# Two streams for the triangular inverses of an RWKV-7 mixer

## The chip, the cores and the metric

The kernel runs on one core of a Trainium2 chip. A core has a matrix engine (TensorE, PE), a vector engine (DVE), a scalar engine (ACT), GpSimd (POOL) and a queue engine (SyncE, SP); each takes its instructions in order and they meet at semaphores. The metric is the device time of one launch in microseconds, the median of three runs: 1651.26 us before the change.

## The reference, cut to what matters

One layer of a recurrent decoder: norm, one input projection, three mixers side by side on the channels, one output projection, norm, MLP, norm. There are 1024 prompt tokens and 8 sample tokens of 1024 channels. The change is in the first mixer, RWKV-7: 6 heads of 64 channels, each with a 64 x 64 state that is updated token by token.

```python
def step(S, inp):
    rt, wt, kt, vt, kkt, at = inp
    sa = jnp.einsum('bhvk,bhk->bhv', S, -kkt)
    S = S * wt[:, :, None, :] + sa[..., None] * (kkt * at)[:, :, None, :] + vt[..., None] * kt[:, :, None, :]
    return S, jnp.einsum('bhvk,bhk->bhv', S, rt)
```

The other two mixers are HGRN2 (6 heads, chunks of 64 tokens) and RG-LRU (a scan over 256 channels).

## The kernel before, in words

Tokens are worked in two halves of 512; the samples go with the second. All dense products take both operands split into two parts, three products for each.

**RWKV-7 in quarters.** Two heads (a pair, 128 channels) by 256 tokens are a *quarter*. There are 12: `PARTS` lists (pair j, half hf, quarter qt) with the half outermost, so quarters 2k and 2k+1 are neighbours in time of one pair, and even and odd quarters alternate. A quarter has four chunks of 64 tokens, and passes through four generators:

- `rw_operands(q)`: decay, removal key, scaled keys and queries (`ee`, `ar`, `kb`, `kbt`, `uv`) and the bonus `bo`. It announces `A2` when done (L565).
- `rw_inverse(q)`: the scores `sc` of the 8 blocks (chunk, head), and the inverse of a triangular 64 x 64 matrix for each, by doubling: five levels, each a product W (from `sc` and `xm`), a copy on ACT to `wm` (L615), a product Y (from `wm` and `ym`), a masked copy into `ym` (L630) and a transpose into `xm` (L634), both on DVE. At the end the product `mv` is copied into `xm` (L641), and `B` is announced. All its products go to two PSUM banks (`ra`).
- `rw_chain(q)`: four steps of the recurrence over the chunks; ends with the copy to `ot` (L700) and announces `C`.
- `rw_finish(q)`: group norm, bonus, gate; the last instruction is at L734, and `P` is announced.

The operands hold back by two announcements of the quarter two before and one of the quarter before:

```python
        if q >= 2:
            yield ("C", q - 2)          # L517
        if q >= 1:
            yield ("sc", q - 1)
        ...
        if q >= 2:
            yield ("P", q - 2)          # L555, just before the bonus
```

**The order of PE's instructions** is the order in which `weave` draws pieces from the generators. It keeps a rough clock of PE, `now`. A generator yields either a time until its next piece can start (the constants D1 to D42) or an announcement that it waits for. Of the ready streams the one that has waited longest is taken; the *filler*, which is the dense work, is taken only where no other stream is ready. Each stream has a priority in `PRI` that goes to the order on the other engines. The streams are the chain, the inverse, the operands, the finish, HGRN2 and the sample step, RG-LRU; each works its quarters one after the other, so only one inverse is under way at a time. The filler `projections()` projects the 27 column tiles of each half in the order of `ORDER`, then does the output projection of the first half, and as much of that of the second (two column tiles over six of eight mixers) as does not need the last mixers; the rest waits until all streams have ended. Six slots hold the projections of the RWKV mixer, three for a pair and a half, which the odd quarter of the pair gives back.

After that come the norm, and the MLP in eight blocks, where PE runs dense products to the end.

Of the kernel before, what the change touches and what calls it, by code (L numbers as in the profile page):

```python
# [9 lines left out]
F32 = mybir.dt.float32  # L10
# [5 lines left out]
PSUM = bass.MemoryType.PSUM  # L16

P = 128
# [22 lines left out]
PRI = [-100, 0, 300, 300, 300, 100, 300]  # L41
# [9 lines left out]
def kernel(ctx: ExitStack, tc: tile.TileContext, i, o):  # L51
# [13 lines left out]
    # The order of the tensor engine's instructions is the order of emission while streams are woven: `now` is a rough  # L65
    # clock of that engine, by which `weave` takes the stream whose operands should be there.
# [15 lines left out]
    def weave(streams, filler, to_the_end=False):  # L82
        """Emits the streams (generators) piece by piece. A stream yields the microseconds until its next piece can
        start, or what it waits for; the filler runs where no other stream is ready."""
# [52 lines left out]
    def x_cols(k, hf):  # L137
        """Where a half of the tokens of a channel tile waits: the mix is written later."""
        return mix[k][:, XC[hf][0]:XC[hf][0] + XC[hf][1]]
# [48 lines left out]
    # lower bound of the forget gate: cumsum(softmax over the depth) minus its first row  # L188
# [13 lines left out]
    # 2 softplus(-lam) = 2 (max(-lam, 0) + log1p(exp(-|lam|))), log1p(e) = 2 atanh(e / (2 + e))  # L202
# [25 lines left out]
    small = ctx.enter_context(tc.tile_pool(name="small", bufs=2))  # L228

    def inv_root(src, n, scale, eps, name):  # L230
        """[128, n] of 1/sqrt(scale * src + eps), src in PSUM."""
        a = small.tile([P, 32], F32, tag="ir", name=f"ir_{name}", bufs=4)
        V.tensor_scalar(a[:, :n], src, scale, eps, op0=ALU.mult, op1=ALU.add)
        rpow(a[:, :n])
        return a

    def head_inv_root(sq, n, name, tag, floor, tmp):
        """sq [128 channels (2 heads), n tokens] -> PSUM [128, n]: 1/sqrt of the sum per head and token."""
# [7 lines left out]
        # on every channel of the head, then channel-major  # L246
# [7 lines left out]
    def load_w(src, name, kt=KT, wpool=wpool, dst=None, parts=1):  # L254
        """One 128-column tile of a weight matrix as its two exact parts."""
# [9 lines left out]
    def dense_steps(out, wh, wl, xh, xl, ks=range(KT), first=True, last=True):  # L265
        """out (PSUM) = W^T x with both operands split in two parts; xh/xl: k -> AP."""
        n = 0
        for k in ks:
            for a, b in ((wh, xh), (wh, xl), (wl, xh)):
                mm(out, a[:, k, :], b(k), start=first and n == 0, stop=last and n == 3 * len(ks) - 1)  # L270
                n += 1
                if n % 2 == 0:
                    yield 0.0
# [16 lines left out]
    def warm(n):  # L290
        """Products that nobody reads: the tensor engine's clock comes up, and stays up, with work."""
# [4 lines left out]
    def norm1(hf):  # L296
        """RMS norm of a half of the tokens; the samples go with the second half. The first half is projected before its
        scale is known, which then falls to the projections; the second is scaled in place."""
# [44 lines left out]
    def xn_cols(hf):  # L343
        """The input of a half in two parts: without the scale of the token in the first, normalised in the second."""
# [8 lines left out]
    def shift_out():  # L353
        """Shift states: the last prompt token and the sample tokens after the norm."""
# [9 lines left out]
    def take(tag):  # L364
        """Waits until a slot of a tag that the projections fill and the mixers empty is free."""
# [10 lines left out]
    def next_w(ask=True):  # L376
        """The next tile of the weights in `ahead`; the one after it is asked for."""
# [5 lines left out]
    # the scale of the first half waits where the mixer of its last projections writes  # L383
# [3 lines left out]
    def project(hf, col, c0, n, bank="big"):  # L387
        """A column tile of a chunk of tokens."""
# [4 lines left out]
    def take_out(hf, out, pt):  # L393
        """A projection to SBUF."""
# [7 lines left out]
    def in_proj(hf, col, evac, shift=False):  # L402
        """Projects a column tile; the next tile's weights (in `ahead`) are asked for before."""
# [14 lines left out]
    def shifted(hf, col, name, out, tag, bufs):  # L418
        """out: pm = P + mu (P_prev - P) of one column tile."""
# [19 lines left out]
    # =========================================================================================  # L439
    # RWKV-7  # L440
    # =========================================================================================
# [37 lines left out]
    def units():  # L479
        """(chunk, head, rows, columns) of the 64 x 64 blocks of a quarter, column halves taking turns."""  # L480
# [4 lines left out]
    def rw_operands(q):  # L485
        """Decay, removal key, bonus and the operands of the scores of a quarter of the tokens of a pair of heads."""
# [15 lines left out]
        # normalised removal key  # L502
        act(t2, k_, AF.Square, scale=vec("kk", j))
        # decay and in-context learning rate
# [12 lines left out]
        if q >= 2:  # L517
            yield ("C", q - 2)
# [3 lines left out]
        ee = rwp.tile([P, NQ, C + 1], F32, tag="ee", name=f"ee_{n}", bufs=2)  # L522
        ar = rwp.tile([P, NQ, 2, C], F32, tag="ar", name=f"ar_{n}", bufs=2)
        kb = rwp.tile([P, NQ // 2, 4, C], F32, tag="kb", name=f"kb_{n}", bufs=1)
        kbt = rwp.tile([P, NQ, P], F32, tag="kbt", name=f"kbt_{n}", bufs=2)
        uv = rwp.tile([P, NQ, P], F32, tag="uv", name=f"uv_{n}", bufs=2)
# [3 lines left out]
        # values, token-major  # L530
# [18 lines left out]
        # token-major [K|B]  # L549
# [18 lines left out]
    def rw_inverse(q):  # L568
        """Scores and Y = (I - A B^T masked)^-T of every (chunk, head), by dyadic blocks."""
# [4 lines left out]
        # scores: rows [K;B] (even chunks) or [B;K] (odd), columns [A|R]  # L574
        sc = rwp.tile([P, 2 * NQ, P], F32, tag="sc", name=f"sc_{n}", bufs=2)
        ym, xm = (w2(nm, n).rearrange("p (u t) -> p u t", t=C) for nm in ("ym", "xm"))
# [21 lines left out]
        for l in range(1, 6):  # L598
            # the last level fills one 32 x 32 block of every unit
            last = l == 5  # L600
            wm = w2("wm", n, 1, f"wm{l}")
# [34 lines left out]
        # what the values of the chunk itself add, for every unit  # L636
# [9 lines left out]
    def rw_chain(q):  # L646
        """The recurrence over the chunks of a quarter; the state is block-diagonal over the two heads."""
# [6 lines left out]
        for c in range(NQ):  # L654
# [38 lines left out]
            if c == NQ - 1:  # L693
                # tokens on the partitions: each head of a token is a row
# [12 lines left out]
    def rw_finish(q):  # L707
        """Group norm per head, bonus, gate."""
# [39 lines left out]
    def rw_sample(j, lora):  # L748
        """One step of a pair of heads for the 8 sample tokens."""
# [9 lines left out]
        # the state with the keys on the partitions  # L759
# [30 lines left out]
        def sums(x, name):  # L790
            """Sums over the rows of a head, on each of its rows."""
# [38 lines left out]
    # =========================================================================================  # L830
    # HGRN2
    # =========================================================================================
# [34 lines left out]
    # queries per head, zero in the rows of the other head  # L867
# [5 lines left out]
    def hg_run(j, hf):  # L873
# [6 lines left out]
        # th becomes 1 - f  # L880
# [15 lines left out]
    def hg_half(j, hf, lf, kin, q, iv, gs):  # L896
# [8 lines left out]
        # within the chunks: dyadic blocks, every exponent at most 0  # L905
# [3 lines left out]
        def scaled(l):  # L909
            """Keys of a level, in their places, and its queries: for each head, zero in the rows of the other."""  # L910
# [18 lines left out]
        def gram(l, kq, rq):  # L929
            """Scores of the second halves of the blocks of a level against its keys."""  # L930
# [11 lines left out]
        # values, token-major  # L942
# [20 lines left out]
        # keys decayed to the end of the chunk, token-major  # L963
# [24 lines left out]
        # what each chunk adds to the state  # L988
# [20 lines left out]
        # outputs, tokens on the partitions  # L1009
# [58 lines left out]
    # =========================================================================================  # L1068
    # RG-LRU
    # =========================================================================================  # L1070
# [22 lines left out]
    def lru(t, hf):  # L1093
# [8 lines left out]
        # GeLU (tanh form), twice its value  # L1102
# [17 lines left out]
        else:  # L1120
            # states: rows [h(last prompt), h(8 samples), last 3 conv rows of the prompt, the samples' new rows]
# [13 lines left out]
        # 2 i x, then 1 - a = T (1 + a) with T = tanh(-log_a / 2)  # L1135
# [6 lines left out]
        # u = sqrt(max(1 - a^2, 1e-12)) i x  # L1142
# [18 lines left out]
    # =========================================================================================  # L1161
    # output projection (its result takes the place of the mix), norm 2, MLP, final norm
    # =========================================================================================
# [4 lines left out]
    # the mixers that end last come last  # L1168
    KS = (0, 1, 3, 4, 6, 7, 2, 5)

    def mixed(k, hf):
        """What a mixer's channel tile of a half waits for."""
# [4 lines left out]
    def out_proj(hf):  # L1177
        """mix -> x + mix W (in its place), its squares added up in acc."""
# [367 lines left out]
```

## Time and profile before

| | us |
|---|---|
| runs, median (lowest to highest) | 1651.26 (1645.96 to 1654.39) |
| profiled execution, span from first to last instruction | 1642.3 |
| its own whole time | not listed |
| PE / PEld busy | 1543.3 / 1316.6 |
| DVE / ACT / POOL busy | 928.2 / 521.4 / 490.2 |

The span is that of the instructions; the time of a run also has what lies around it. PE's ends are modelled, so a busy PE is not one at its peak; PEld is the loading of the weights, beside the products. The mixers and their dense filler take the first 912 us, the MLP the rest. A row of the timeline has the start in us from the first instruction, the duration, engine, line, operation, what is written from what is read, shapes and count, and in brackets how long the engine had been idle before it and what ended that. A row of the waits has who waited for whom, then the total in us, the number of times and the longest.

### The profile page before, as it was taken

To read this page: it belongs to the slowest core of one execution; us is meant where nothing else is said; L and a number is where in the kernel's file an instruction comes from. 1 tells how busy PE (TensorE), PEld (TensorE's weight loads), DVE (VectorE), ACT (ScalarE), POOL (GpSimd) and SP (SyncE) were. 2 spreads that over 40 slices of the span, in tenths; PEclk is the share of its full clock that TensorE was granted. 3 is DMA by queue.
4 is the path that set the end of the run, shared out by engine and by line. 5 is a ranking of instruction groups with operands and counts; after the bars stand their busy time and mean duration, and the time that the engine had idled before them with its cause. 6 is when DMAs were issued, how large, how long until landed. Compare 5 with 4: busy or idle time off the path is not lost. (4 is left out here: it accounts for less than half of the span.)

```text
span 1642.3 us, 29129 instructions
## 1 busy us (share of the span) xinstructions
PE 1543.3 (94%) x12158; PEld 1316.6 (80%) x12158; DVE 928.2 (57%) x1816; ACT 521.4 (32%) x1210; POOL 490.2 (30%) x441
## 2 busy tenths in 40 slices
PE   7869898999899988999999999999999999999997
PEld 5647666678788877776788898898989989898887
DVE  7686867775667667777676543433343343433334
ACT  3342523542434333533343312212131312122122
POOL 4684324343334533633554301101020101111001
PEclk8979999999899989989999999999999999999998
DMA  5201111111011111111233111111111111111012
GB/s 192 88 27 52 40 40 40 40 40 46 33 40 40 59 36 53 47 48 40 86 102 126 55 55 46 47 44 52 39 52 49 42 51 40 52 39 46 27 33 104
DMA packets 32755, 89.76 MB, mean 55 GB/s; under 512 B 4688, under 2 KB 4976, under 8 KB 32624
## 3 DMA queue, kind: packets, MB, share of 16 engines
q1 hardware_dynamic: 29808, 79.61, 15.1%
q0 software_dynamic: 2672, 8.27, 1.5%
q8 instruction: 95, 1.56, 0.4%
q14 instruction: 36, 0.29, 0.1%
q10 hardware_dynamic: 144, 0.04, 0.0%
HBM read 81.73 MB, written 6.17 MB: 54 GB/s over the span
## 5 line engine op out<-in xcount | busy, mean ns | idle before, releaser
L262 POOL TENSOR_TENSOR wl_w<-raw_w,wh_w 128x1024 fp32r<-128x1024 f32 x32 | 76.9, 2404 | 577.0 <-ACT wh_w L261 577.0
L73 PE MATMUL in<-xl,wh_in 128*128 128x512 f32 (+3 forms) x648 | 227.7, 351 | 5.7 <-DVE xl L351 5.6
L73 PE MATMUL in<-xh,wl_in 128*128 128x512 f32 (+3 forms) x648 | 227.5, 351 | 0.0
L73 PE MATMUL in<-xh,wh_in 128*128 128x512 f32 (+3 forms) x648 | 225.8, 348 | 0.1
L73 PE MATMUL dn<-hh,wh_w 128*128 128x264 f32 (+2 forms) x696 | 223.6, 321 | 1.9 <-DVE mix L1434 1.8
L73 PE MATMUL dn<-hl,wh_w 128*128 128x264 f32 (+2 forms) x696 | 222.7, 320 | 0.0
L73 PE MATMUL dn<-hh,wl_w 128*128 128x264 f32 (+2 forms) x696 | 222.1, 319 | 0.0
L1434 DVE TENSOR_TENSOR mix<-mix,dn 128x512 f32<-128x512 f32 (+2 forms) x192 | 97.7, 512 | 195.4 <-PE dn L73 195.4
L261 ACT ACTIVATE wh_w<-raw_w 128x512 fp32r<-128x512 f32 (+1 forms) x90 | 70.6, 784 | 308.0 <-PE dn L73 259.2
L262 POOL TENSOR_TENSOR wl_in<-raw_in,wh_in 128x1024 fp32r<-128x1024 f32 x52 | 126.0, 2423 | 87.5 <-ACT wh_in L261 87.2
L1363 DVE SCALAR_TENSOR_TENSOR rl<-up,rl 128x512 f32<-128x512 f32 (+2 forms) x96 | 49.6, 516 | 177.8 <-ACT rl L1362 177.8
L73 PEld LDWEIGHTS in<-xl,wh_in 128*128 128x128 f32 x648 | 130.9, 202 | 21.8 <-DVE xl L351 8.3
L73 PE MATMUL up<-nxh,wh_w 128*128 128x264 f32 (+1 forms) x512 | 144.6, 282 | 0.0
L73 PE MATMUL up<-nxh,wl_w 128*128 128x264 f32 (+1 forms) x512 | 144.4, 282 | 0.0
L73 PE MATMUL up<-nxl,wh_w 128*128 128x264 f32 (+1 forms) x512 | 144.1, 281 | 0.1
L73 PEld LDWEIGHTS in<-xh,wl_in 128*128 128x128 f32 x648 | 130.9, 202 | 15.6 <-issue 5.1
L73 PEld LDWEIGHTS in<-xh,wh_in 128*128 128x128 f32 x648 | 130.4, 201 | 15.2 <-issue 3.9
L73 PEld LDWEIGHTS dn<-hh,wh_w 128*128 128x128 f32 x696 | 131.0, 188 | 13.8 <-DVE mix L1434 3.2
L73 PEld LDWEIGHTS dn<-hl,wh_w 128*128 128x128 f32 x696 | 130.9, 188 | 10.1
L73 PEld LDWEIGHTS dn<-hh,wl_w 128*128 128x128 f32 x696 | 130.8, 188 | 10.0
L1365 DVE TENSOR_TENSOR hl<-rl,hh 128x512 fp32r<-128x512 f32 (+2 forms) x96 | 82.8, 862 | 51.0 <-ACT hh L1364 51.0
L73 PE MATMUL up<-nh,wl_w 128*128 128x512 f32 x256 | 101.6, 397 | 0.2 <-POOL wl_w L262 0.2
(434 smaller groups left out, 3289.7 us busy)
## 6 DMA issues: line engine op xcount, KB each, us to landing
raw_in<-in_w_in SPq DMA_DIRECT2D x53, 512.0 KB, 3.3
raw_w<-in_w SPq DMA_DIRECT2D x32, 512.0 KB, 3.3
raw_w<-in_w SPq DMA_DIRECT2D x64, 256.0 KB, 2.6
raw_out<-in_w_out SPq DMA_DIRECT2D x16, 512.0 KB, 3.4
out_y_prompt<-yt SPq DMA_DIRECT2D x16, 256.0 KB, 2.0
mix<-in_xt SPq DMA_DIRECT2D x8, 264.0 KB, 5.1
xr<-in_xt POOLq DMA_DIRECT2D x8, 260.0 KB, 4.2
mix<-in_xt SPq DMA_DIRECT2D x8, 256.0 KB, 4.7
```

Source lines behind the costliest of these rows:

```text
L73: PE.matmul(out, lhsT, rhs, start=start, stop=stop)
L261: act(wh[:, ks], raw[:, ks], AF.Copy)
L262: (G if kt == KT and name not in FIRST else V).tensor_tensor(wl[:, ks], raw[:, ks], wh[:, ks], op=ALU.subtract)
L1363: V.scalar_tensor_tensor(rl[:, :n], pt[:, :n], 0.0, rl[:, :n], op0=ALU.max, op1=ALU.mult)
L1365: V.tensor_tensor(hl[:, c0:c0 + n], rl[:, :n], hh[:, c0:c0 + n].bitcast(F32), op=ALU.subtract)
L1434: V.tensor_tensor(x2[m][:, c0:c0 + n], x2[m][:, c0:c0 + n], pt[:, :n], op=ALU.add)
```

## The change

The inverse becomes two streams, one for the even quarters and one for the odd ones, with one more entry in `PRI`. The tiles that a quarter holds from its operands to its chain get three buffers in place of two, the scratch tile `wm` two in place of one, and the operands wait for the chain of three quarters before. The wait for `P` of two quarters before and the two buffers of `bo` stay. To make room, the scratch that DMAs issued by GpSimd use is set to 2048 bytes a partition. The comments are taken out (not shown).

```diff
-PRI = [-100, 0, 300, 300, 300, 100, 300]
+PRI = [-100, 0, 0, 300, 300, 300, 100, 300]
...
-        if q >= 2:
-            yield ("C", q - 2)
+        if q >= 3:
+            yield ("C", q - 3)
         if q >= 1:
             yield ("sc", q - 1)
         yield D6
-        ee = rwp.tile([P, NQ, C + 1], F32, tag="ee", name=f"ee_{n}", bufs=2)
-        ar = rwp.tile([P, NQ, 2, C], F32, tag="ar", name=f"ar_{n}", bufs=2)
+        ee = rwp.tile([P, NQ, C + 1], F32, tag="ee", name=f"ee_{n}", bufs=3)
+        ar = rwp.tile([P, NQ, 2, C], F32, tag="ar", name=f"ar_{n}", bufs=3)
         kb = rwp.tile([P, NQ // 2, 4, C], F32, tag="kb", name=f"kb_{n}", bufs=1)
-        kbt = rwp.tile([P, NQ, P], F32, tag="kbt", name=f"kbt_{n}", bufs=2)
-        uv = rwp.tile([P, NQ, P], F32, tag="uv", name=f"uv_{n}", bufs=2)
+        kbt = rwp.tile([P, NQ, P], F32, tag="kbt", name=f"kbt_{n}", bufs=3)
+        uv = rwp.tile([P, NQ, P], F32, tag="uv", name=f"uv_{n}", bufs=3)
...
-        sc = rwp.tile([P, 2 * NQ, P], F32, tag="sc", name=f"sc_{n}", bufs=2)
-        ym, xm = (w2(nm, n).rearrange("p (u t) -> p u t", t=C) for nm in ("ym", "xm"))
+        sc = rwp.tile([P, 2 * NQ, P], F32, tag="sc", name=f"sc_{n}", bufs=3)
+        ym, xm = (w2(nm, n, 3).rearrange("p (u t) -> p u t", t=C) for nm in ("ym", "xm"))
...
-            wm = w2("wm", n, 1, f"wm{l}")
+            wm = w2("wm", n, 2, f"wm{l}")
...
-        weave([each(rw_chain, *NP), each(rw_inverse, *NP), each(rw_operands, *NP), each(rw_finish, *NP), hgrn(),
+        weave([each(rw_chain, *NP), each(rw_inverse, *NP[0::2]), each(rw_inverse, *NP[1::2]), each(rw_operands, *NP), each(rw_finish, *NP), hgrn(),
                each(lru, *((t, hf) for hf in range(2) for t in range(2)))], dense_work)
...
-    nc = bacc.Bacc("TRN2", target_bir_lowering=False, num_devices=1)
+    nc = bacc.Bacc("TRN2", target_bir_lowering=False, num_devices=1, dynamic_dma_scratch_size=2048)
```

## The prediction

> **What bounds the kernel now.** I read the page's busy line first, then the busy time by stages, then the position of single steps of the recurrence in the timeline, and last the chain of waits of TensorE. The stages are cut where the two quarters of a head pair begin and end.
>
> ```profile
> PE 1543.3 (94%) x12158; PEld 1316.6 (80%) x12158; DVE 928.2 (57%) x1816; ACT 521.4 (32%) x1210; POOL 490.2 (30%) x441
> ...
> 85.00:150.00 65.00, 50.92 (x363) 37.73 (x362) 49.70 (x63) 24.72 (x42) 43.64 (x41) 0.84 0.13 41
> 150.00:267.00 117.00, 106.45 (x986) 76.41 (x986) 86.07 (x183) 46.26 (x121) 40.75 (x38) 0.96 0.13 41
> 267.00:380.00 113.00, 105.15 (x1116) 82.67 (x1114) 85.19 (x189) 46.99 (x130) 42.27 (x41) 0.97 0.12 40
> 380.00:500.00 120.00, 110.91 (x1149) 95.60 (x1146) 76.19 (x185) 41.79 (x127) 45.71 (x44) 0.91 0.13 41
> 500.00:621.00 121.00, 111.04 (x1211) 96.38 (x1210) 84.08 (x203) 42.97 (x129) 53.03 (x52) 0.92 0.14 46
> 621.00:741.00 120.00, 109.94 (x1220) 92.72 (x1220) 88.37 (x211) 50.80 (x137) 53.19 (x52) 0.96 0.14 46
> 741.00:843.00 102.00, 98.08 (x828) 73.98 (x824) 70.59 (x139) 37.67 (x102) 46.27 (x39) 0.97 0.22 75
> 843.00:912.00 69.00, 64.17 (x457) 60.97 (x456) 51.13 (x77) 30.28 (x58) 37.00 (x30) 0.95 0.30 100
> sum 827.00, PE 756.65 PEld 616.46 DVE 591.33 ACT 321.48 POOL 361.86; mean PE 94.58 PEld 77.06 DVE 73.92 ACT 40.19 POOL 45.23
> ```
>
> The columns are length, then busy time of PE, PEld, DVE, ACT and POOL, then the granted clock and the DMA's share and rate. Only the first 912 us can change; what follows is the MLP, untouched. In the 827 us from 85 to 912 PE is busy for 756.65: it idles for 70. Adding length times (1 - clock) over the eight rows gives 10.4 + 4.7 + 3.4 + 10.8 + 9.7 + 4.8 + 3.1 + 3.5 = 50 us of clock not granted. So what can be won in this phase, without removing work, is 120 us at most, and the question is which part of it the second stream touches.
>
> Next, the recurrence. B(q) is the end of a quarter's inverse (L641), A2(q) the end of its operands (L561), C(q) the end of its chain (L700), P(q) the end of its finish (L734). Single rows of the timeline:
>
> ```profile
> 125.95 0.42 DVE L561 TENSOR_TENSOR bo<-bonus,pm_v 128x256 f32<-128x256 f32 x1 [5.83 <-PE bonus L73]
> 150.69 0.37 ACT L641 COPY xm<-mv 128x256 f32<-128x256 f32 x1 [1.24 <-PE mv L73]
> 154.54 0.69 DVE L585 TENSOR_TENSOR sc<-sc,cmask 128x512 f32<-128x512 f32 x1 [0.51 <-PE sc L73]
> 187.58 0.22 ACT L700 ACTIVATION_READ_ACCUMULATOR ot<-ch 128x1 f32 x1
> 206.44 0.37 ACT L641 COPY xm<-mv 128x256 f32<-128x256 f32 x1 [1.20 <-PE mv L73]
> ...
> 433.76 0.48 DVE L734 SCALAR_TENSOR_TENSOR mix<-mix,vt,gate 128x256 f32<-128x256 f32 x1 [0.85 <-PE gate L73]
> 439.44 0.42 DVE L561 TENSOR_TENSOR bo<-bonus,pm_v 128x256 f32<-128x256 f32 x1
> 439.49 0.35 ACT L641 COPY xm<-mv 128x256 f32<-128x256 f32 x1
> 443.18 0.69 DVE L585 TENSOR_TENSOR sc<-sc,cmask 128x512 f32<-128x512 f32 x1
> 499.83 0.37 ACT L641 COPY xm<-mv 128x256 f32<-128x256 f32 x1 [0.45 <-PE mv L73]
> 542.33 0.22 ACT L700 ACTIVATION_READ_ACCUMULATOR ot<-ch 128x1 f32 x1
> 550.75 0.48 DVE L734 SCALAR_TENSOR_TENSOR mix<-mix,vt,gate 128x256 f32<-128x256 f32 x1 [1.47 <-PE gate L73]
> 555.02 0.42 DVE L561 TENSOR_TENSOR bo<-bonus,pm_v 128x256 f32<-128x256 f32 x1
> 555.64 0.37 ACT L641 COPY xm<-mv 128x256 f32<-128x256 f32 x1 [1.77 <-PE mv L73]
> 842.42 0.48 DVE L734 SCALAR_TENSOR_TENSOR mix<-mix,vt,gate 128x256 f32<-128x256 f32 x1 [0.79 <-PE gate L73]
> ```
>
> The second block is one turn of the loop: P(4) 434.2, A2(6) 439.9, B(6) 500.2, C(6) 542.6, P(6) 551.2, A2(8) 555.4. The reader is to see two things in it. A quarter's operands end 4 to 6 us after the finish of the quarter two before, and they end at the same time as the inverse of the quarter before (439.9 against B(5) at 439.8; 555.4 against B(7) at 556.0). So two limits hold at once: the serial inverse, and the loop P(q-2) to P(q), 117 us in this turn.
>
> Last, does PE end with the recurrence or with its dense work?
>
> ```profile
> 839.98 0.28 PE L73 MATMUL out<-mh,wl_out 128*128 128x264 f32 x1
> 840.33 0.78 PE L77 MATMUL oT<-ident,ot 128*128 128x128 f32 x2
> 841.69 0.70 PE L73 MATMUL gate<-pm_xg,gup 128*128 128x256 f32 x2 [0.58 <-DVE mix L729]
> 843.63 0.39 PE L73 MATMUL out<-mh,wh_out 128*128 128x256 f32 x1 [0.46 <-ACT mh L1187]
> ```
>
> The dense filler that may run ahead of the last quarter ends at 840.3, the last finish at 842.9. Both end together. The filler is emitted only where no mixer is ready, so PE's work is conserved: a recurrence that ends earlier leaves more dense work behind it.
>
> **The change part by part.** *Three buffers, and C(q-3) in place of C(q-2).* This removes one of the waits of the operands. But L555 still waits for P(q-2), because the bonus tile keeps two buffers, and P(q-2) comes after C(q-2). The steps between the two waits (values transposed, scales, the copies to token-major) move forward, A2 does not. What that saves: the token-major transposes now come right behind the gate in the same single PSUM bank and wait for its evacuation.
>
> ```profile
> PE oT L77 <- DVE ot L722: 16.2, 8, 3.7
> PE kbt L77 <- DVE mix L734: 6.6, 7, 2.0
> PE W L73 <- DVE xm L634: 5.3, 2, 4.9
> PE Y L73 <- ACT wm L615: 2.7, 3, 2.3
> PE W L73 <- DVE xm L596: 1.6, 1, 1.6
> 541.25 0.45 DVE L634 STREAM_TRANSPOSE xm<-ym 128x256 f32<-128x256 f32 x1
> 542.65 0.68 PE L73 MATMUL W<-xm,sc 64*64 64x64 f32 x16
> ```
>
> The second row is that wait: 6.6 us in seven pieces. It should go nearly whole: -6 us, the range 0 (the bank is taken by another user) to -6.6. What is late next is the bonus product, behind the same gate, but a planned delay later than the transposes were.
>
> *The second stream.* Inverse q can start at A2(q) although inverse q-1 runs. Because of the wait for P(q-2) the streams hardly find each other ready: in the loop above A2 falls on B(q-1). The exception is q = 1: operands at 126.4, B(0) at 151.1. Inverse 1 can start 24.7 us earlier. Its chain must wait for chain 0, which ends at 187.8, where it now waits for B(1) at 206.8: so 19 us at least of the 24.7 reach the chain. After that the odd quarters keep this lead, as each turn is the same loop, and the odd quarter 11 is the last: P(11) at 842.9 - 19 to 25, say 821. The even quarters gain nothing.
>
> What is that worth? By conserved work only what PE loses at the meeting at 840 to 844: the filler ends 2.6 us before the finish, and two short gaps of 0.58 and 0.46 follow: -3 us. The work that covers the other 19 us is the output projection of the first half, which now stands beside quarter 11 and would then follow it. If that cover were gone the whole 22 us would count; that is the first rival.
>
> [...]
>
> *The price of overlap.* Per turn the two inverses overlap for some 22 of 57 us. Nothing in the trace shows two at once. The nearest row from below is PE's own wait inside the inverse, 9.6 us in all (5.3 + 2.7 + 1.6), which another stream's launches might fill: -9.6. From above: 48 W and 60 Y launches, 39% of them overlapped, each one evacuation and transpose of the other stream late (0.30 + 0.45 us): +32 us. A launch is late only where its data has no slack, and the last two rows show slack: the transpose ends at 541.70, its product starts at 542.65. I take +2, near the lower end. The two PSUM banks of the inverses turn round as before: of any three launches in a row two belong to one stream, and those stand a planned delay of 2 us apart.
>
> *Clock.* The clock is lost near idle stretches; 10 us less idle out of 70 takes in proportion 50/70 of 10 = 7 us. I count 3 of them, with 0 and 7 as ends.
>
> *Third buffers, smaller DMA scratch, copies.* No instruction is added. POOL issues the same DMAs:
>
> ```profile
> xr<-in_xt POOLq DMA_DIRECT2D x8, 260.0 KB, 4.2
> ```
>
> The residual rows of the output projection are the only POOL transfers in bulk. They are asked for with the tile's weights, ahead of 24 products, so even twice 4.2 us would be hidden; if that cover were gone each of the 16 would cost up to 4. I take 0.
>
> **Sum.** -6 - 3 + 2 - 3 = -10 us. The profiled span is 1642.3 us; its own whole time is not listed, and the three runs have their median at 1651.26, 9 us above that span, part of it outside the span and part spread (1645.96 to 1654.39). The difference is put on the median: 1641 us.
>
> **Rivals.**
> - *Latency decides.* The phase follows the loop: 22 us from the odd lead and 6 from the transposes, 1651 - 28 = 1623. For it speaks that 120 us of idle and unclocked time lie in the phase; against it that dense products fill PE up to 840.3. Chance 0.18, 1615 to 1632.
> - *Nothing to interleave.* P(q-2) keeps the streams apart, what the early quarter 1 gains is lost again by the projections (the operands of quarter 10 start when its key is projected, next row), and small shifts of order cancel the 6 us: 1648. Chance 0.22, 1644 to 1656.
>
> ```profile
> 642.32 0.51 ACT L503 ACTIVATE t<-pm_k,vt 128x256 f32<-128x256 f32 x1 [3.32 <-DVE pm_k L435]
> ```
>
> - *The overlapped inverses stall PE, slower.* Place: the launches of W behind the transpose and of Y behind the copy, while both streams run. DVE is 591 of 827 us busy, and PE takes its instructions strictly in the written order, so everything behind a late launch waits, dense work too. Price: half of the +32 worked out above, 16, with no other gain: 1667. It decides once an overlapped launch is late by over 0.24 us on the mean (10 us over 42 launches). Against it stands the slack of 0.95 us. Chance 0.18, 1658 to 1675.
> - The forecast itself: chance 0.42, 1633 to 1650.
>
> **How the numbers follow.** A measurement of this kernel tells about 0.5% from no change, 8 us: faster is under 1643, slower over 1659.5. Faster: the first rival and 0.26 of the forecast's 0.42, 0.44. Slower: the stall, 0.18. The rest, 0.38, is the same. The range leaves out the outer half of the first rival and the outer half of the stall: 1624 to 1665; the forecast's own range is 1633 to 1650.
>
> **What would show it.** Right: the wait of the token-major transposes for the gate is gone; the first row of L585 for quarter 1 stands near 130; the odd quarters lead by about 20 us and the even ones by none; P(11) near 821, with dense products from there without gaps. Wrong: A2(q) no longer tied to P(q-2); PE's waits of W and Y above 20 us in sum; a recurrence that ends at 843 as before; or a phase that ends well before 900 although the recurrence gained 20 us, which would say that latency was the limit.

## The result

The changed kernel takes 1671.81 us (median of four runs, 1665.38 to 1673.65) against 1649.08 us before (1645.96 to 1654.39): ratio 1.0132, 95% interval 1.0103 to 1.0162. It is slower by some 23 us, where 10 us less were forecast. Its profiled execution took 1673.65 us for a span of 1671.9, so only 1.8 us lie around a span; the profiled execution of the kernel before, with a span of 1642.3, was one of its quicker ones, and that of the changed kernel the longest of its four. So the two traces lie 30 us apart and not 23.

The page's busy line after the change, and then the stage from 60 us to the first product of the MLP (889.4 us before, 920.2 us after), once for the kernel before and once for the changed one. Columns as in the prediction: length, busy time of PE, PEld, DVE, ACT, POOL, the granted clock, DMA.

```profile
PE 1566.2 (94%) x12158; PEld 1337.3 (80%) x12158; DVE 930.3 (56%) x1816; ACT 522.2 (31%) x1210; POOL 489.5 (29%) x441
```

```profile
60.00:889.40 829.40, 756.44 (x7267) 613.37 (x7267) 589.37 (x1236) 317.78 (x832) 361.21 (x329) 0.94 0.16 51
```

```profile
60.00:920.20 860.20, 779.44 (x7267) 634.00 (x7267) 591.64 (x1236) 318.88 (x832) 359.92 (x327) 0.90 0.15 49
```

The same 7267 products take 30.8 us longer. DVE, ACT and POOL do the same work (589 and 592, 318 and 319, 361 and 360 us). PE's idle time goes from 73.0 to 80.8 us, 8 more. Its busy time goes from 756 to 779, 23 more, and the granted clock beside it falls from 0.94 to 0.90: the products themselves ran slower. The trace's record of the granted clock holds only whole and half: after 60 us there are 16 half-clock stretches of 105.8 us in all before, and 22 of 163.8 us after. Half of that is lost, if a product at half clock takes twice its time: 52.9 and 81.9 us, 29 more. (In unbroken runs of both traces the dense products of 512 columns start 0.427 us apart at half clock and 0.233 at whole, those of 264 columns 0.220 and 0.122, 1.8 times; by that the loss would be 47 and 73 us, 26 more.) With half counted, in this pair of traces the clock is 29 us longer and the waiting 8; what is left is 703.5 us before and 697.5 after, 6 less (3 less at 1.8 times), which these rows don't explain.

The executions on record have their mean granted clock beside their span. The span times one less the clock is lost: 66 us on the mean over 73 executions of the kernel before (59 to 74; two far longer ones, of 1874 and 4802 us, are left out), 85 over the four of the changed one (80 to 89). Their mean times are 1648.3 and 1670.7 us, so some 18 of the 22 us between them are clock. One and the same order loses more in one execution than in another.

The recurrence after the change (B, A2, C, P as in the prediction):

```profile
129.16 0.42 DVE L561 TENSOR_TENSOR bo<-bonus,pm_v 128x256 f32<-128x256 f32 x1 [5.87 <-PE bonus L73]
132.45 0.69 DVE L585 TENSOR_TENSOR sc<-sc,cmask 128x512 f32<-128x512 f32 x1
159.61 0.37 ACT L641 COPY xm<-mv 128x256 f32<-128x256 f32 x1
184.53 0.37 ACT L641 COPY xm<-mv 128x256 f32<-128x256 f32 x1 [1.29 <-PE mv L73]
197.86 0.22 ACT L700 ACTIVATION_READ_ACCUMULATOR ot<-ch 128x1 f32 x1
207.88 0.48 DVE L734 SCALAR_TENSOR_TENSOR mix<-mix,vt,gate 128x256 f32<-128x256 f32 x1
214.26 0.42 DVE L561 TENSOR_TENSOR bo<-bonus,pm_v 128x256 f32<-128x256 f32 x1 [0.28 <-PE bonus L73]
322.32 0.48 DVE L734 SCALAR_TENSOR_TENSOR mix<-mix,vt,gate 128x256 f32<-128x256 f32 x1 [0.71 <-PE gate L73]
329.01 0.41 DVE L561 TENSOR_TENSOR bo<-bonus,pm_v 128x256 f32<-128x256 f32 x1
688.00 0.48 DVE L734 SCALAR_TENSOR_TENSOR mix<-mix,vt,gate 128x256 f32<-128x256 f32 x1
697.62 0.42 DVE L561 TENSOR_TENSOR bo<-bonus,pm_v 128x256 f32<-128x256 f32 x1 [0.35 <-PE bonus L73]
869.19 0.48 DVE L734 SCALAR_TENSOR_TENSOR mix<-mix,vt,gate 128x256 f32<-128x256 f32 x1 [3.39 <-PE gate L73]
```

Inverse 1 starts 22 us earlier (its first scores at 132.45, 154.54 before) and ends at 184.9 (206.8). Yet A2(2) still comes 6 us behind P(0), A2(4) 6 us behind P(2), A2(10) 10 us behind P(8), as the wait at L555 dictates, and the first product of inverse 2 starts (217.7) 33 us after inverse 1 has ended. The streams overlap in the odd quarters alone. Inverse 0, which now has inverse 1 beside it, ends at 160.0 (151.1 before), and chain 0 at 198.1 (187.8). The last finish is at 869.7, not 842.9.

PE's waits after the change, from 85 us on, and below them the first of these rows as it was before:

```profile
PE ch L73 <- DVE rh L664: 18.7, 11, 5.2
PE pb_kk L77 <- DVE t L247: 10.5, 3, 8.9
PE oT L77 <- DVE ot L722: 10.3, 5, 3.2
PE W L73 <- DVE xm L634: 8.4, 4, 4.8
PE W L73 <- DVE xm L596: 3.8, 2, 2.3
```

```profile
PE ch L73 <- DVE rh L664: 5.4, 6, 1.8
```

The wait of the token-major transposes for the gate (6.6 us) has no row any more. The wait for the chain's sum `rh` went from 5.4 to 18.7 us. The inverses' own waits, of W and Y, are 12.2 us against 9.6.

**How the clock falls.** One place of the changed kernel: PE's instructions, then the busy time of the stage up to the fall and of the next, and in the last fence that of the dense projection alone.

```profile
568.42 0.28 PE L73 MATMUL in<-xl,wh_in 128*128 128x264 f32 x1
568.63 0.70 PE L73 MATMUL pw<-pm_wa,waup 64*128 64x256 f32 x2
569.26 1.10 PE L73 MATMUL hso<-hq,hsst 64*64 64x1 f32 x32
570.29 0.34 PE L73 MATMUL ch<-uv,kbt 128*64 128x64 f32 x4
570.46 0.38 PE L73 MATMUL ch<-st,ar 128*64 128x128 f32 x2
570.68 0.39 PE L73 MATMUL ch<-uv,sc 128*64 128x64 f32 x4
571.00 1.26 PE L73 MATMUL sc<-ar,kb 64*128 64x128 f32 x8
```

```profile
568.50:571.90 3.40, 3.40 (x54) 2.85 (x52) 1.19 (x5) 0.47 (x1) 1.03 (x3) 1.00 0.16 61
571.90:582.10 10.20, 10.20 (x45) 9.13 (x43) 6.89 (x16) 2.06 (x4) 7.30 (x5) 0.50 0.24 75
```

```profile
568.50:571.90 3.40, 0.20 (x2) 0.00 (x0) 0.00 (x0) 0.00 (x0) 1.00 0.16 61
```

PE was busy for all of the 3.40 us, but with small mixer products and 0.20 us of dense ones; then the clock is halved for 10.2 us, in which PE again counts as wholly busy. A busy column does not show this loss, only the clock column does.

This place is not the usual one. I cut both traces into the 3.41 us windows at whose borders the recorded clock changes, and took for each the share that the dense products fill, each product counted with the time between two starts in an unbroken run of the trace (0.12 us for 256 to 272 columns, 0.23 for 512). Before, 16 of the 82 full-clock windows with a share under 0.4 were followed by a fall, and none of the 129 others; after, 21 of 74 and none of 129. In most of these windows PE also waited. Of the 37 before a fall, 30 had over 1.26 us of idle time (37%), three had 0.40 to 0.94 us, and four, two in each trace, had 0.03 us at most. The other way round, 30 of the 40 windows with over 37% of idle time were followed by a fall (11 of 18 before, 19 of 22 after), and 4 of the 84 that had a share under 0.4 while PE was busy for over 95%. So in these traces a fall goes with few dense products, and nearly always with waiting in the same window; small products alone seldom do it.

The half-clock stretches after 60 us last 3.4 us (6 before, 7 after), 6.8 (7 and 10), 10.2 (1 and 2) or 13.7 (2 and 2), and one after lasts 23.9: each a whole number of such windows. Only three of the 37 windows before a fall were idle throughout, and the one above held no idle time, so in these traces a fall did not need an idle window.

### The profile page after: what moved, and what is told of

It reads as the page before. It is cut to its first block, busy times and chain, and to the rows that moved or that the text cites. A ratio compares the mean times of both kernels' runs of the same rounds, so it can differ in the third digit from the quotient of the medians.

```text
span 1671.9 us, 29111 instructions
## 1 busy us (share of the span) xinstructions
PE 1566.2 (94%) x12158; PEld 1337.3 (80%) x12158; DVE 930.3 (56%) x1816; ACT 522.2 (31%) x1210; POOL 489.5 (29%) x441
## 5 line engine op out<-in xcount | busy, mean ns | idle before, releaser
L73 PE MATMUL in<-xh,wh_in 128*128 128x512 f32 (+3 forms) x648 | 230.2, 355 | 0.1
```

What stands on the lines that cost most here:

```text
L73: PE.matmul(out, lhsT, rhs, start=start, stop=stop)
```

## The experiments

Theories at the start: *clock* (the second stream bunches the mixers, and the clock falls), *chain* (the chain's sums come late on DVE and lengthen the loop), *reorder* (any other order of the pieces loses, as the planned delays suit the order of before; the stream has no price of its own). All times are medians; "phase" is the span from 60 us to the MLP, and "lost" is PE's idle time plus half of the half-clock time in it.

**e1, the buffers alone.** One stream and one `wm`, the buffers, the wait and the scratch of the change:

```diff
-        if q >= 2:
-            yield ("C", q - 2)
+        if q >= 3:
+            yield ("C", q - 3)
 ... ee, ar, kbt, uv, sc, ym, xm: bufs 2 -> 3; dynamic_dma_scratch_size=2048
```

> The kernel before with the three buffers, the wait for C(q-3) and the smaller scratch, but one stream of inverses. Clock theory (the loss is TensorE clock, taken where mixer products bunch up without dense ones between; it needs the second stream): within 0.5% of before, 1641 to 1657 us, half-clock time up to 912 us within 15 us of before's 106. Reorder theory (any other order of the pieces loses what the delays were set for): 1658 to 1670. Step of the prediction: the wait of the token-major transposes for the gate (6.6 us) is gone here too.

1639.88 us, ratio 0.9955 (0.9934 to 0.9976): the fastest kernel of all, and below both ranges. PE's order differs here too, from 171 us on, and nothing is lost: the reorder theory, as it was put, does not hold. The token-major wait falls to 0.3 us, PE's idle time by 5.5 us, the clock stays (109.2 us at half).

```profile
60.00:882.70 822.70, 755.25 (x7266) 614.01 (x7267) 590.46 (x1236) 317.83 (x832) 359.97 (x327) 0.93 0.16 51
```

**e2, the second stream alone.**

```diff
-PRI = [-100, 0, 300, 300, 300, 100, 300]
+PRI = [-100, 0, 0, 300, 300, 300, 100, 300]
-each(rw_inverse, *NP),
+each(rw_inverse, *NP[0::2]), each(rw_inverse, *NP[1::2]),
 ... wm: bufs 1 -> 2; dynamic_dma_scratch_size=2048
```

> The kernel before with the second stream, two scratch tiles for it and the smaller DMA scratch, but two buffers and the wait for C(q-2) as before. Clock theory: most of the loss is here, 1662 to 1675 us, with 40 us or more of added half-clock time. Reorder theory: 1658 to 1670 as well. Chain theory (the chain's sums come late on DVE behind the other streams' work, so each turn of the loop is longer): as after, with TensorE's waits for rh above 12 us. If the third buffers carry the loss instead: 1645 to 1655.

1666.23 us, ratio 1.0110 (1.0072 to 1.0147). At these delays the loss comes with the stream, not with the buffers. But it is not the same loss: idle 91.7 us (+19), half-clock 126.3 (+20.5, so 10 lost), less than the 40 that the clock theory wanted; and PE's wait for `rh` is 4.6 us, less than before, against the chain theory.

**e3, a control: one planned delay.** The constant stands at three announcements of each quarter, A2, B and P.

```diff
-L_EV, ... = 1.59, ...
+L_EV, ... = 1.7, ...
```

> A control: the kernel before with one planned delay changed from 1.59 to 1.70 us, which only reorders pieces; no stream, no buffer is added. Reorder theory: slower by 0.7 to 1.5%, 1660 to 1675 us. Clock and chain theory: within 0.4% of before, 1643 to 1656.

1676.27 us, ratio 1.0170 (1.0133 to 1.0207). No stream, no buffer, and a loss larger than that of the change, just above the reorder theory's range: idle +20, half-clock 143.4.

```profile
60.00:921.40 861.40, 768.55 (x7272) 623.28 (x7270) 594.87 (x1238) 319.61 (x832) 360.51 (x330) 0.92 0.15 49
```

**e4, forced dense pieces in the changed kernel.** `bare` adds up weave's clock over mixer pieces since the last piece of filler:

```diff
             s = min(c)[2]
+            if bare > 1.0 and fill in live and any(x[2] is fill and x[0] <= now[0] for x in r):
+                s = fill
```

> The changed kernel, where weave takes a piece of the dense filler after every 1.0 us (by its own clock) of mixer pieces without one, so that mixers can't bunch. Clock theory: the half-clock time up to the MLP falls from 164 us to under 120 and the time to 1640 to 1655 us. Chain theory: no gain or a loss, as the forced pieces stand in the chain's way: 1670 to 1690. Reorder theory: anywhere from 1650 to 1675, without a bond to the half-clock time.

1645.81 us, ratio 0.9995 (0.9955 to 1.0035): 26 us gained, and half-clock time of 92.2 us, the least of all traces (its executions go from 1637.62 to 1661.53, and the traced one took 1640.32). For itself that speaks for the clock theory, and it lies below the range of the reorder theory. A single wait of 21.8 us from 96 us on is in it: PE waits for a copy on DVE (L252), which first stands behind GpSimd's scaling of the second half's input (12.7 us from 91.9) and then behind other work on DVE. First the phase, then the wait:

```profile
60.00:887.20 827.20, 748.60 (x7271) 603.14 (x7270) 580.52 (x1238) 318.61 (x832) 360.78 (x328) 0.94 0.16 51
```

```profile
PE pb_kk L77 <- DVE t L252: 32.9, 5, 21.8
```

**e5 and e6, the changed kernel with other delays; e7, the kernel before with the second of them.** e5 as in e3; e6 and e7, cut from the line of constants:

```diff
-D20 = 1.6
+D20 = 1.75
```

> The changed kernel with the same planned delay changed from 1.59 to 1.70 us. Reorder theory (the loss is that of any reordering away from the order that the delays were set for, the second stream has no price of its own): as likely faster as slower than the changed kernel, between 1645 and 1685 us, and not above the 1676 us that the same edit gave without the stream by more than 10 us. Stream theory (two streams bunch the mixers whatever the delays): 1680 us or more, since both losses add up (1672 + 27 = 1699).

> The changed kernel with another planned delay changed, that between the group norm's transposes and the gate, from 1.60 to 1.75 us. Reorder theory: 1645 to 1685 us, with a mean over the changed kernel's three orders that lies within 10 us of the mean over the one-stream orders disturbed in the same way. Stream theory: 1665 or more.

> Control: the kernel before with that second delay changed from 1.60 to 1.75 us. Reorder theory: slower by 0.7% or more, 1660 to 1680 us. If the first control was an accident of one delay: within 0.5%, 1641 to 1657.

e5: 1652.80 us, ratio 1.0018 (1.0002 to 1.0033). e6: 1661.46, 1.0085 (1.0058 to 1.0112). e7: 1659.54, 1.0079 (1.0052 to 1.0105); it just misses the 1660 expected at least. The delay that cost the kernel before 27 us gains the changed one 19: the losses do not add, and the stream theory (1680 or more) falls. Over the three settings the changed kernel takes 1662.0 us on the mean, and the kernel before (1649.08, e3 and e7) 1661.6.

**e8, forced pieces in the kernel before**, as in e4 from 120 us of weave's clock on.

> The kernel before, with a piece of the dense filler forced after every 1.0 us of mixer pieces without one, from 120 us of weave's clock on (earlier it made a queue of VectorE and GpSimd work wait 22 us). Clock theory (dense pieces between the mixers keep the clock and the waits down, in any order): 1625 to 1642 us with half-clock time under 100 us. Reorder theory: it is one more order away from the delays' own, 1655 to 1680 us.

1660.77 us, ratio 1.0070 (1.0042 to 1.0097). The half-clock time stays (102.4), the idle time grows by 13 us. Forced pieces do not help in every order; e4 looks like a good order, not a cure.

**e9, the wait that holds the streams apart.**

```diff
-        if q >= 2:
-            yield ("P", q - 2)
+        if q >= 3:
+            yield ("P", q - 3)
-        bo = w2("bo", n)
+        bo = w2("bo", n, 3)
```

> The changed kernel with the wait that holds its streams apart loosened: three buffers for the bonus tile and P(q-3) in place of P(q-2) (the DMA scratch goes to 1024 bytes for the room). Loop reading of the prediction: the operands of quarter q no longer end 4 to 8 us behind P(q-2) but ahead of it, two inverses run at once in most quarters, and quarter 10's finish comes 15 us or more earlier than in the changed kernel. Conserved work: the time stays among the other orders, 1640 to 1675 us, although the recurrence runs ahead. Latency theory (the first rival): 1625 us or less.

1668.78 us, ratio 1.0105 (1.0076 to 1.0135). Rows of e9:

```profile
199.31 0.42 DVE L561 TENSOR_TENSOR bo<-bonus,pm_v 128x256 f32<-128x256 f32 x1
210.47 0.48 DVE L734 SCALAR_TENSOR_TENSOR mix<-mix,vt,gate 128x256 f32<-128x256 f32 x1
237.15 0.42 DVE L561 TENSOR_TENSOR bo<-bonus,pm_v 128x256 f32<-128x256 f32 x1
324.16 0.47 DVE L734 SCALAR_TENSOR_TENSOR mix<-mix,vt,gate 128x256 f32<-128x256 f32 x1
338.14 0.42 DVE L561 TENSOR_TENSOR bo<-bonus,pm_v 128x256 f32<-128x256 f32 x1
669.95 0.51 ACT L503 ACTIVATE t<-pm_k,vt 128x256 f32<-128x256 f32 x1 [1.08 <-DVE pm_k L435]
828.84 0.48 DVE L734 SCALAR_TENSOR_TENSOR mix<-mix,vt,gate 128x256 f32<-128x256 f32 x1
```

A2(2) now ends at 199.7, ahead of P(0) at 211.0: the wait at L555 was what tied them. But two inverses still run at once in the odd quarters alone, not in most. A2(4) ends 14 us behind P(2), and quarter 10 starts its operands only at 670, when its key is projected (642 before), so P(10) is at 829.3, the 830.9 of the changed kernel less 1.6, not the 15 us expected. There the projections hold the recurrence, and these are the filler that PE gets to last. The time stays among the other orders; but as the recurrence did not end earlier, this run does not test what an earlier end would bring.

**e10 and e11, the buffers alone with the two delays; e12, with forced pieces.** The edits are those of e3, e6 and e8 on e1.

> The buffers alone with the delay changed from 1.59 to 1.70 us; the kernel before with that delay took 1676 us. If the buffers have a price of their own (the wait of the token-major transposes for the gate is gone): 5 to 15 us less than that, 1661 to 1671 us, and no such wait above 1 us in all. If their gain alone was one of order: anywhere from 1640 to 1680.

> The buffers alone with the second delay changed from 1.60 to 1.75 us; the kernel before with it took 1660 us. Price of their own: 1645 to 1655 us. Order alone: anywhere from 1640 to 1680.

> The buffers alone with the forced pieces of filler from 120 us on. With the kernel before the forced pieces gave 1661 us, with the changed one (from the start on) 1646. If forced pieces help wherever the token-major wait is gone: 1620 to 1636 us, the fastest of all. If they are but another order: 1640 to 1670.

e10: 1676.54 us, ratio 1.0158 (1.0134 to 1.0182), the same as e3 without the buffers. e11: 1653.44, 1.0030 (1.0015 to 1.0046), 6 less than e7. The token-major wait is gone in both. With e1 (-9 to the kernel before) the buffers gave -9, 0 and -6 us under equal delays. e12: 1685.53, 1.0217 (1.0195 to 1.0240), the slowest of all and above both ranges: with forced pieces the buffers cost 25 us (e8 1660.77). So a gain of their own, the size of the wait of 6.6 us, can't be told from the scatter.

```profile
60.00:932.20 872.20, 779.50 (x7274) 627.71 (x7273) 602.07 (x1238) 318.21 (x832) 356.25 (x328) 0.91 0.15 49
```

**e13 to e16, two more delays with one stream and with two.** The delay behind W from 2.08 to 2.20 us (e13 buffers alone, e14 changed kernel), and one in the chain from 1.40 to 1.50 (e15, e16).

> One stream with the new buffers; the delay behind the product W set from 2.08 to 2.20 us. Reorder theory: anywhere from 1640 to 1680 us, and TensorE's idle time plus the clock not granted up to the MLP explains it: the rest of the phase stays within 696 to 708 us. Stream theory (a price of 15 us or more of the second stream): 15 us or more under e14.

> The changed kernel with the same delay, 2.20 us. Reorder theory: 1640 to 1680, as likely under e13 as over it, the rest of the phase 696 to 708 us. Stream theory: 15 us or more above e13.

> One stream with the new buffers; the delay inside the chain set from 1.40 to 1.50 us. Reorder theory: 1640 to 1680, rest of the phase 696 to 708 us. Stream theory: 15 us or more under e16.

> The changed kernel with the same delay, 1.50 us. Reorder theory: 1640 to 1680, as likely under e15 as over it. Stream theory: 15 us or more above e15.

e13: 1672.68 us, ratio 1.0130 (1.0057 to 1.0202), of four executions from 1655.57 to 1676.81. e14: 1648.07, 1.0005 (0.9987 to 1.0022). e15: 1656.76, 1.0057 (1.0035 to 1.0078). e16: 1660.27, 1.0078 (1.0050 to 1.0106).

| delays | one stream, new buffers | two streams, new buffers |
|---|---|---|
| as in the code | 1639.88 (e1) | 1671.81 (the change) |
| 1.59 to 1.70 | 1676.54 (e10) | 1652.80 (e5) |
| 1.60 to 1.75 | 1653.44 (e11) | 1661.46 (e6) |
| 2.08 to 2.20 | 1672.68 (e13) | 1648.07 (e14) |
| 1.40 to 1.50 | 1656.76 (e15) | 1660.27 (e16) |
| mean | 1659.9 | 1658.9 |

The second stream costs -1 us on the mean of five settings; the five differences (+32, -24, +8, -25, +4) scatter so that the mean is known to some 11 us (standard error). With five settings the 95% interval is some 30 us either way, so a mean price of 20 us is not excluded; but the sign turns with the delay, so the 23 us of the result are not a price common to all settings. All six changes of a delay with one stream (e3, e7, e10, e11, e13, e15) made the kernel slower than with the delays in the code, all four with two streams made it faster: the delays in the code look set for the order of one stream, and for two streams they are a poor draw.

**All together.** PE's time in the phase, from the busy column and the clock's record:

| kernel | phase | idle | half-clock | rest |
|---|---|---|---|---|
| e1 | 822.7 | 67.5 | 109.2 | 700.6 |
| before | 829.4 | 73.0 | 105.8 | 703.5 |
| e14 | 838.2 | 79.6 | 112.6 | 702.3 |
| e9 | 858.9 | 83.7 | 153.6 | 698.4 |
| after | 860.2 | 80.8 | 163.8 | 697.5 |
| e3 | 861.4 | 92.9 | 143.4 | 696.9 |
| e12 | 872.2 | 92.7 | 160.4 | 699.3 |

Rest is the phase less idle less half of the half-clock time. Over all 18 traces it lies between 696.0 and 707.8 us while the phase goes from 822.7 to 872.2, and the phase follows idle plus lost clock with a correlation of 0.99. PE's work is fixed; the order, and within one order the execution, decides how much is waited and how often the clock is halved.

## Why the prediction was wrong

*What held.* That L555 keeps the operands tied to P(q-2), so that the streams hardly meet (the rows above, and e9 when it is loosened). That the token-major wait goes: its row is gone. That the clock is lost near idle stretches (30 of 37 falls above). That the inverses hardly stall PE: their waits grew by 2.6 us, +2 was taken.

*What was not decided.* Conserved work against the first rival, latency. That the rest is the same in 18 orders says that PE's own work is fixed, not what the phase waits for. In all 18 traces the first product of the MLP comes 44 to 57 us after the last finish (46.5 before, 50.5 after): the time and the end of the recurrence moved together, and no run ended the recurrence well ahead of the dense work. (That product stands at 889.4 us before, so the prediction's stages, cut at 912, reach into the MLP.)

*What failed.* First the term of the clock: -3 us was taken, with 0 and -7 as ends, and it was +29 in the traces, some +18 over all executions. It was worked out as a share of the idle time, which was to fall by 10 and rose by 8. Nor is it a fixed share: e14, the changed kernel and e6 idle for 79.6, 80.8 and 81.5 us, with half-clock times of 112.6, 163.8 and 163.8. How the waits lie together counts as well: 22 windows had over 37% of idle time and 19 of them were followed by a fall, against 18 and 11 before. Second, and behind it, the step *no instruction is added*, and the sum of local terms altogether: each wait was priced in the order of before, as if all else stood. The second stream moves PE's order from the 444th product on (127.9 us before), and with it the waits: `rh` +13 us, the transposes of the finish -6, new falls of the clock. The control e3 shows what such a move is worth by itself: a tenth of a microsecond in one constant costs 27 us. The range allowed one way to be slower, overlapped inverses that stall PE, and that rival was wrong too: the loss was elsewhere. A range fit for a new draw of the order had to reach from some 1640 to 1685.

Third, the lead of the odd quarters. 19 us at least were to reach the last finish; 22 reached B(1), 8.5 reached P(1) (253.5 against 262.0). Chain 1 waits for chain 0, which the prediction left at 187.8; beside inverse 1, inverse 0 ended 9 us later, 3 of them from its operands, and chain 0 at 198.1. That belongs to the second stream and not to the draw of the order: from A2 to B inverse 0 takes 69.7 to 70.5 us in all ten traces with one stream, and 71.7 to 75.6 in all eight with two. So a price of overlap was paid here, by the even inverse, though not in PE's waits. Up to P(7) the odd quarters kept 4 to 9 us of lead and the even ones were 8 to 12 late; P(10) was 34 us late, behind a stage (621 to 741 us) in which the granted clock was 0.84, not 0.96.

*What stays open.* Why the order of the changed kernel, of all, has six more half-clock stretches. Forced dense pieces took the half-clock time to 92 us there (e4), but helped in no other order (e8, e12), so that it can be steered by such pieces is not shown. What would come of a recurrence that ends early is open too. Whether the second stream, with delays set anew for it, would beat e1 was not tried.

## What to carry to other kernels

Where one engine's instructions are written out in an order that planned delays decide, a structural change is also a new draw of that order: change one delay by some 6 to 9% in both versions, several times, before a difference of 1 or 2% is put down to the structure. Before sizing a change that lets work start earlier, look for every wait that stands before it; here a second wait left in place, for a small tile with two buffers, kept the operands where they were, though seven other tiles had a third buffer. And where a phase is dense filler between small steps, read the clock column beside the busy one, and over several executions: the busy share was 91% before and after, the granted clock 0.94 and 0.90.

## What the runs showed of the hardware that was not expected

The clock of TensorE was halved after 3.4 us in which it was never idle, but had only 0.20 us of dense products (568.5 to 571.9 above). That was rare: of the 84 full-clock windows with a dense share under 0.4 and PE busy for over 95%, 4 were followed by a fall. Windows that were idle in part did it far more often, 30 of the 40 with over 37% of idle time, and three only of the 37 windows before a fall were idle throughout. Windows whose dense share was at least 0.4 were never followed by a fall, 258 of 258 in the two traces.

The same kernel, run again, lost between 59 and 74 us to the clock over 73 executions, so one trace of each version can overstate a difference: 29 us here, where the executions give some 18.
